# A two-layer hybrid decoder trunk on one core: first loads, the first norm, and the order of the first products

## The chip, the cores and the metric

The kernel runs on one core of a Trainium2 chip. The metric is the time of one execution in microseconds on the device. The kernel before took 1389.82 us, the median of three runs (1389.7 to 1390.5). A core has five engines that run side by side, each with its own queue of instructions in a fixed order: TensorE (PE in the profile; its weight loads are PEld), VectorE (DVE), ScalarE (ACT), GpSimd (POOL) and SyncE (SP), which here issues nearly all transfers from main memory. Semaphores tie them together.

## The reference

A sequence of 512 tokens of width 1024 is normalised and goes through two layers. Each is a mixer (attention with eight query heads in two key/value groups, beside a short gated convolution) and a feed-forward block, dense in layer 0 and with eight experts in layer 1. Cut to what matters here:

```python
def layer_norm(x, g, b):
    mu = jnp.mean(xf, -1, keepdims=True)
    var = jnp.mean(jnp.square(xf - mu), -1, keepdims=True)
    return ((xf - mu) * lax.rsqrt(var + LN_EPS) * g + b).astype(x.dtype)
...
def hybrid_mixer(h, w_in, ...):
    z = h @ w_in
    q, kc, vc, ks, vs, kw, vw, gates, u, bg, cg = jnp.split(z, offsets, axis=-1)
    kc_c = compress(kv(kc), ...)
    vc_c = compress(kv(vc), ...)
    ...
def reference(x, ln_in_g, ln_in_b, ...):
    h = layer_norm(x, ln_in_g, ln_in_b)
    for l in range(DEPTH):
        m = hybrid_mixer(h, ...)
        h = layer_norm(ALPHA * h + m, ln1_g[l], ln1_b[l])
        f = swiglu(h, ...) if l % 2 == 0 else moe_swiglu(h, ...)
        h = layer_norm(ALPHA * h + f, ln2_g[l], ln2_b[l])
    return h
```

Of z the change touches kc and vc (keys and values that are compressed in blocks) and ks and kw (keys of the selected blocks and of the window). These four, 128 columns each, are the "first projections" of a layer.

## The kernel before

The activations h stay on chip as four blocks of 128 tokens (`NT` = 4) by 1024. Every wide product is made of three: an operand x is split into a high half xh (a reduced format that TensorE multiplies quickly) and a low half xl, the rest; a weight w likewise into whi and wlo. Then x w is xh whi + xl whi + xh wlo, summed in one bank of PSUM. `split` (L136) makes the weights' halves: whi on ScalarE (L142), wlo on DVE or, for the first projections of layer 0, on POOL (L143). `split_t` (L175) transposes one block of h on TensorE into a bank of the kind "tr" (L183), and takes xh from it on ScalarE (L187) and xl on DVE (L188).

There are eight banks of PSUM: two "mm", two "tr", three "s" and one "po". A tile that takes a bank again waits until the bank's last reader is done. Weights come in through a ring of three buffers, "stage"; the halves whi and wlo have rings of four each. The program is written in order, but a scheduler places the instructions on the engines' queues; what it made of them is seen in the rows of the section on the change.

Head (L60 to L105, and `run`, L1092): `setup` issues, in this order, blocks 0 and 1 of x, ln_in_g, ln_in_b, the first weights `st0` (the 256 columns of kc and vc, 1 MB), and blocks 2 and 3 of x. `mixer` adds `st2` (ks and kw) behind them. Then small constants are made (an identity for the transposes, masks). `run` normalises the four blocks: two `bn_stats` of 512 columns on DVE (`ln_stats`, L159), their aggregate (L166), a square root on ScalarE (L167), a reciprocal (L168), and two passes over the block, (x - mean) g (L925) and times 1/sigma plus b (L926), then `split_t`.

First projections (`proj_first`, L209): four weights, four banks (mm, mm, s, s). The tokens are taken in two halves of 256 (`th`), so that work can start when two of the four blocks are ready. In a half, one projection after the other, and within it for each of the eight slices of 128 rows (`KD` = 8) the three products xh whi, xl whi, xh wlo: 24 matmuls of 256 columns a projection, 96 a half, 192 in all. It is called in three places: the mixer of layer 0, the first step of the feed-forward block of layer 0 (L600; there the four are two pairs of gate and up columns), and the mixer of layer 1.

After it, in `mixer` (L252), the four banks `pf[0]` to `pf[3]` are read. pf[0] and pf[1] (kc, vc) go into the tiles e_0 and e_1: for each of two groups g and each of two offsets, two copies of 64 partitions from ScalarE (r = 0, L302) and two from DVE (r = 1, L304). pf[2] and pf[3] (ks, kw) become ks on ScalarE (L282, and L285 for the other half of the partitions) and the rest kl on DVE, eight instructions of 64x512 (L284). In layer 0 `columns` (L119) transposes a tile of constants on TensorE into an mm bank (L122), and copies it to `cols` (L124). Then come q's projections (`proj_t`, 24 matmuls of 512 columns each, mm banks) and `compress` (L361), whose first products (L373) read e_0.

Of the kernel before, what the change touches and what calls it, by code (L numbers as in the profile page):

```python
# [7 lines left out]
F32 = mybir.dt.float32  # L8
F32R = mybir.dt.float32r
BF = mybir.dt.bfloat16  # L10
F16 = mybir.dt.float16
I32 = mybir.dt.int32
AF = mybir.ActivationFunctionType
OP = mybir.AluOpType
# [3 lines left out]
S, D, NT, KD = 512, 1024, 4, 8  # L18
# [28 lines left out]
C_KC, C_VC, C_KS, C_VS, C_KW, C_VW, C_G, C_U, C_B, C_C = 512, 640, 768, 896, 1024, 1152, 1280, 1304, 1816, 2328  # L47


class Trunk:  # L50
# [9 lines left out]
    def setup(self):  # L60
        nc, t = self.nc, self.t
        self.const = self.pool("const")
        self.state = self.pool("state")
        self.ring = self.pool("ring", 2)
        self.small = self.pool("small", 4)
        c = self.const
        self.h = self.state.tile([128, NT, D], F32, name="h")
        self.gb = self.ring.tile([128, 2, D], F32, name="stage", bufs=3)
        for tt in range(NT):
            nc.sync.dma_start(self.h[:, tt], t["x"][0, tt * 128:(tt + 1) * 128])  # L70
            if tt == 1:
                self.ln_load(self.gb, t["ln_in_g"], t["ln_in_b"])
                self.st0 = self.block([128, KD, 256], lambda s: [(s, self.win(0, C_KC, 256))])
        self.eps = c.tile([128, 1], F32, name="eps")
        nc.vector.memset(self.eps, EPS)
        early = self.state.tile([128, 2, 128], I32, name="xl")
        jp, jc = early[:, 0], early[:, 1].rearrange("p (t n) -> p t n", t=NT)
        nc.gpsimd.iota(jp, pattern=[[1, 128]], base=0, channel_multiplier=-1)
        self.ident = c.tile([128, 128], F32, name="ident")
        nc.vector.tensor_scalar(self.ident, jp, 0.0, None, op0=OP.is_equal)  # L80
        self.identb = c.tile([128, 128], BF, name="identb")
        nc.vector.tensor_copy(self.identb, self.ident)
        self.cneg = c.tile([128, 128], BF, name="cneg")
        nc.vector.tensor_scalar(self.cneg, jp, 0.0, NEG, op0=OP.is_gt, op1=OP.mult)
        self.fold = c.tile([128, 64], F32, name="fold")
        nc.vector.tensor_tensor(self.fold, self.ident[:, 0:64], self.ident[:, 64:128], op=OP.add)
        nc.gpsimd.iota(jc, pattern=[[-128, NT], [16, 32]], base=31, channel_multiplier=-1)
        self.nneg = c.tile([128, NT, 32], BF, name="nneg")
        nc.vector.tensor_scalar(self.nneg, jc, 0.0, NEG, op0=OP.is_gt, op1=OP.mult)
        self.nkeep = c.tile([128, NT, 32], BF, name="nkeep")  # L90
        nc.vector.tensor_scalar(self.nkeep, jc, 0.0, None, op0=OP.is_le)
        self.nkeep8 = c.tile([128, 8, 8], BF, name="nkeep8")
        nc.gpsimd.memset(self.nkeep8, 0.0)
        for e in range(1, NE):
            nc.gpsimd.memset(self.nkeep8[:, e, 0:e], 1.0)
        self.before = c.tile([128, 128], BF, name="before")
        nc.vector.tensor_scalar(self.before, jp, 0.0, None, op0=OP.is_gt)
        self.ones = c.tile([128, 128], BF, name="ones")
        nc.vector.memset(self.ones, 1.0)
        self.slots = c.tile([128, CAP], F16, name="slots")  # L100
        nc.gpsimd.iota(self.slots, pattern=[[1, CAP]], base=1, channel_multiplier=0, allow_small_or_imprecise_dtypes=True)
        self.toks = c.tile([128, NT], F16, name="toks")
        nc.gpsimd.iota(self.toks, pattern=[[128, NT]], base=0, channel_multiplier=1, allow_small_or_imprecise_dtypes=True)
        self.dump = c.tile([128, 2], F32, name="dump")
        nc.gpsimd.iota(self.dump, pattern=[[CH, 2]], base=S, channel_multiplier=1, allow_small_or_imprecise_dtypes=True)  # L105

    def columns_load(self, ip):

        nc, t = self.nc, self.t
        rows = ip.tile([128, 128], F32, name="rows")  # L110
        nc.gpsimd.memset(rows, 0.0)
        nc.sync.dma_start(rows[0:64], t["cmp_pos"].rearrange("l k (c r) d -> (l k c) (r d)", r=2))
        nc.sync.dma_start(rows[64:88], t["conv_w"].rearrange("l k (j p) -> (l k j) p", p=128))
        nc.sync.dma_start(rows[88:96], t["cmp_b1"].rearrange("l k (m p) -> (l k m) p", p=128))
        for r in range(2):
            nc.sync.dma_start(rows[96:100, r * 64:(r + 1) * 64], t["cmp_b2"].rearrange("l k d -> (l k) d"))
        return rows
# [43 lines left out]
    def ln_rows(self, x, st, gb):  # L161

        nc = self.nc
        m = x.shape[0]
        mv, rs = (self.small.tile([128, n], F32, name=name)[0:m] for name, n in (("mv", 2), ("rs", 1)))
        nc.vector.bn_aggr(mv, st)  # L166
        nc.scalar.activation(rs, mv[:, 1:2], AF.Sqrt, bias=self.eps[0:m])  # L167
        nc.vector.reciprocal(rs, rs)  # L168
        self.rows_scaled(x, mv[:, 0:1], rs, gb)
        return mv  # L170
# [38 lines left out]
    def proj_first(self, sts, engs=(None,) * 4):  # L209

        ws = [tuple(self.split(st, 128, eng=eng)) for st, eng in zip(sts, engs)]
        ps = [self.psum(tag) for tag in ("mm", "mm", "s", "s")]
        for th in range(2):
            q = slice(th * 256, th * 256 + 256)
            for (hi, lo), p in zip(ws, ps):
                self.mm3(p[:, q], lambda k: (hi[:, k], lo[:, k], self.xh[:, k, q], self.xl[:, k, q]), 0, KD)
        return ps

    def rows_out(self, nk, load, act, gb, after):
# [872 lines left out]
    def run(self):  # L1092
        self.ps = self.pool("ps", 1, PSUM)
        self.setup()
        gb = self.gb
        for tt in range(NT):
            for half in range(2):
                self.ln_stats(tt, half)
            self.ln_norm(tt, gb)
            self.split_t(tt)  # L1100
        for l in range(DEPTH):
            if l % 2 == 0:
                self.mixer(l, self.split_t)
                self.ffn(l)
            else:
                rp = self.pool("route%d" % l)
                dp = self.ctx.enter_context(self.tc.tile_pool(name="moed%d" % l, bufs=1, space=bass.MemoryType.DRAM))
                self.hbuf = dp.tile([S, D], F32, name="hbuf")
                self.abuf = dp.tile([S + CAP, D], F32, name="abuf")
                self.route(l, rp)  # L1110

                def after(tt):
                    for rows in (self.hbuf, self.abuf):
                        self.nc.gpsimd.dma_start(rows[tt * 128:(tt + 1) * 128], self.h[:, tt])
                    self.route_tile(tt)
                self.mixer(l, after)
                self.moe(l)
# [32 lines left out]
```

## Time and profile before

| | us |
|---|---|
| median of the runs | 1389.82 (1389.7 to 1390.5) |
| the profiled execution | 1391.8 |
| its span, first to last instruction | 1389.8 |
| TensorE busy | 1339.5 |
| DVE busy | 867.3 |
| ScalarE busy | 670.0 |
| POOL busy | 75.1 |
| layer 0: first transposes start | 11.91 |
| layer 0: first products start | 17.05 |
| layer 0: second half of tokens starts | 34.53 |
| layer 0: first projections end, columns' transpose starts | 45.89 |
| layer 0: q's projections start | 46.48 |
| layer 1: q's projections start | 669.89 |

The profile is of one execution, and the times in it count from the start of its span. Matmuls are pipelined: the step from one start to the next (0.12 us for 256 columns) is what one costs, not its own duration (0.28).

### The profile page before, as it was taken

To read this page: it belongs to the slowest core of one execution; us is meant where nothing else is said; L and a number is where in the kernel's file an instruction comes from. 1 tells how busy PE (TensorE), PEld (TensorE's weight loads), DVE (VectorE), ACT (ScalarE), POOL (GpSimd) and SP (SyncE) were. 2 spreads that over 40 slices of the span, in tenths; PEclk is the share of its full clock that TensorE was granted. 3 is DMA by queue.
4 is the path that set the end of the run, shared out by engine and by line. 5 is a ranking of instruction groups with operands and counts; after the bars stand their busy time and mean duration, and the time that the engine had idled before them with its cause. 6 is when DMAs were issued, how large, how long until landed. Compare 5 with 4: busy or idle time off the path is not lost.

```text
span 1389.8 us, 27646 instructions
## 1 busy us (share of the span) xinstructions
PE 1339.5 (96%) x11888; PEld 1181.5 (85%) x11888; DVE 867.3 (62%) x1249; ACT 670.0 (48%) x951; POOL 75.1 (5%) x81
## 2 busy tenths in 40 slices
PE   5999999999999999999999999999999999999974
PEld 5887888898888888888888878889999999999974
DVE  7567665843333332228567665769787788778876
ACT  3575544332322322122565444236777677668761
POOL 3000000000000000000000000101101140011010
PEclk9999999999999999999999999999999999999986
DMA  7442021232322322234442021679999999999961
GB/s 249 128 121 62 31 61 61 91 122 72 110 92 90 121 92 91 91 107 110 130 122 62 32 61 61 211 270 321 327 356 334 323 332 389 337 363 353 343 236 75
DMA packets 135810, 241.16 MB, mean 174 GB/s; under 512 B 10810, under 2 KB 80538, under 8 KB 135684
## 3 DMA queue, kind: packets, MB, share of 16 engines
q1 hardware_dynamic: 131444, 225.28, 47.5%
q0 software_dynamic: 4240, 14.07, 3.7%
q8 instruction: 94, 1.54, 0.5%
q14 instruction: 32, 0.26, 0.1%
HBM read 227.74 MB, written 11.68 MB: 172 GB/s over the span
## 4 chain that ended last, share of the span: by engine, by line
PE 91%; DVE 4%; DMA 2%; ACT 1%; issue 1%; SPq 0%; POOL 0%; POOLq 0%; ACTq 0%
PE mm L198 46%; PE s L198 17%; PE tr L198 11%; PE po L481 3%; PE s L499 2%; PE s L465 2%; PE s L373 1%; PE po L198 1%; PE tr L465 1%; PE tr L499 1%; DVE h L925 1%; PE tr L183 1%; DVE h L926 1%; PE mm L677 1%; PE po L475 1%
## 5 line engine op out<-in xcount | busy, mean ns | idle before, releaser
L198 PEld LDWEIGHTS <-whi 128*128 128x128 f16 x4224 | 342.8, 99 | 2.9 <-issue 2.4
L142 ACT ACTIVATE whi<-stage 128x1024 fp32r<-128x1024 f32 x122 | 127.9, 1058 | 304.8 <-PE mm L198 181.7
L143 DVE TENSOR_TENSOR wlo<-stage,whi 128x1024 fp32r<-128x1024 f32 x118 | 143.7, 1223 | 196.6 <-ACT whi L142 194.4
L198 PE MATMUL mm<-xh,whi 128*128 128x512 f32 (+1 forms) x672 | 257.4, 383 | 0.3 <-DVE e L304 0.3
L198 PE MATMUL mm<-xh,wlo 128*128 128x512 f32 (+1 forms) x672 | 253.0, 377 | 0.4 <-DVE wlo L143 0.4
L198 PE MATMUL mm<-xl,whi 128*128 128x512 f32 (+1 forms) x672 | 252.3, 376 | 0.0
L825 DVE SCALAR_TENSOR_TENSOR wlo<-estage,whi 128x1536 f16<-128x1536 f32 (+4 forms) x106 | 201.6, 1919 | 35.2 <-ACT whi L824 34.9
L198 PEld LDWEIGHTS <-wlo 128*128 128x128 f16 x2112 | 208.6, 99 | 13.2 <-DVE wlo L825 13.2
L824 ACT ACTIVATE whi<-estage 128x1536 f16<-128x1536 f32 (+4 forms) x106 | 170.6, 1613 | 68.8 <-PE s L198 28.0
L198 PEld LDWEIGHTS mm<-xh,wlo 128*128 128x128 f32 x672 | 127.1, 189 | 24.0 <-DVE wlo L143 0.6
L198 PEld LDWEIGHTS mm<-xh,whi 128*128 128x128 f32 x672 | 127.6, 190 | 21.6 <-issue 1.3
L198 PEld LDWEIGHTS mm<-xl,whi 128*128 128x128 f32 x672 | 127.3, 189 | 21.1
L198 PE MATMUL tr<-eh,wlo 128*128 128x128 f16 (+6 forms) x704 | 136.2, 228 | 8.3 <-DVE wlo L825 8.3
L198 PE MATMUL s<-ehh,wlo 128*128 128x128 f16 (+6 forms) x704 | 134.7, 228 | 4.5 <-DVE wlo L825 4.5
L198 PE MATMUL tr<-eh,whi 128*128 128x128 f16 (+6 forms) x704 | 136.3, 229 | 0.0
L198 PE MATMUL tr<-el,whi 128*128 128x128 f16 (+6 forms) x704 | 136.2, 228 | 0.0
L198 PE MATMUL s<-ehh,whi 128*128 128x128 f16 (+6 forms) x704 | 134.7, 228 | 1.1 <-ACT ehh L865 1.1
L198 PE MATMUL s<-ehl,whi 128*128 128x128 f16 (+6 forms) x704 | 134.6, 228 | 1.1 <-DVE ehl L866 1.1
L198 PE MATMUL mm<-eh,whi 128*128 128x128 f16 (+6 forms) x704 | 132.7, 226 | 0.0
L198 PE MATMUL mm<-el,whi 128*128 128x128 f16 (+6 forms) x704 | 132.6, 226 | 0.0
L198 PE MATMUL mm<-eh,wlo 128*128 128x128 f16 (+6 forms) x704 | 132.6, 226 | 0.0
L825 DVE SCALAR_TENSOR_TENSOR wlo<-stage,whi 128x1536 f16<-128x1536 f32 (+5 forms) x56 | 103.0, 1842 | 23.2 <-ACT whi L824 22.2
(302 smaller groups left out, 2220.7 us busy)
## 6 DMA issues: line engine op xcount, KB each, us to landing
estage<-in_moe_wd_dram SPq DMA_DIRECT2D x29, 1024.0 KB, 7.7
stage<-in_w_in_dram SPq DMA_DIRECT2D x32, 512.0 KB, 5.1
estage<-in_moe_wu_dram SPq DMA_DIRECT2D x21, 768.0 KB, 10.5
estage<-in_moe_wg_dram SPq DMA_DIRECT2D x18, 768.0 KB, 7.1
stage<-in_ffn_wg_dram SPq DMA_DIRECT2D x11, 1024.0 KB, 5.2
stage<-in_ffn_wu_dram SPq DMA_DIRECT2D x11, 1024.0 KB, 5.2
stage<-in_ffn_wd_dram SPq DMA_DIRECT2D x11, 1024.0 KB, 4.8
stage<-in_moe_wd_dram SPq DMA_DIRECT2D x11, 1024.0 KB, 9.4
```

The costliest lines, as they stand in the source:

```text
L142: nc.scalar.activation(h, st, AF.Copy)
L143: (eng or nc.vector).tensor_tensor(o, st, h.bitcast(F32), op=OP.subtract)
L183: nc.tensor.transpose(p[:, k * 128:(k + 1) * 128], self.h[:, tt, kk * 128:(kk + 1) * 128], self.ident)
L198: self.nc.tensor.matmul(p, a, b, start=first and n == 0, stop=last and n == total - 1, skip_group_check=shared)
L373: nc.tensor.matmul(ph[r:r + 64, 0:256], e2[kv][:, c].rearrange("p g n -> p (g n)"), w1s[c // 8][:, c % 8], start=c < 2, stop=c > 13, skip_ ...
L465: nc.tensor.transpose(q[:, k * 128:k * 128 + 128], flat[:, c:c + 128], self.ident)
L475: nc.tensor.matmul(po, vbd[r], pct[r, la // 2], start=True, stop=False, skip_group_check=True)
L481: nc.tensor.matmul(po[g * 64:g * 64 + 64, i * 128:i * 128 + 128], v[:, j, c:c + 64], flat[:, k:k + 128], start=False, stop=lbr == 1 and j ...
L499: nc.tensor.matmul(sp[:, wide[i]], qs[:, a, g, qi[i]], keys[:, br, g, 0:wide[i].stop - wide[i].start], start=keys is ks and i == blocks[0] ...
L677: self.nc.tensor.matmul(p, self.h[:, tt, k * 128:k * 128 + 128], self.oh32[:, tt], start=tt == 0 and k % 3 == 0, stop=tt == NT - 1 and (k ...
L824: nc.scalar.activation(hi[:, c], st[:, c], AF.Copy, scale=WS)
L825: self.low = nc.vector.scalar_tensor_tensor(lo[:, c], st[:, c], WS, hi[:, c], op0=OP.mult, op1=OP.subtract)
```

## The change

Four things are done. The loads move from `setup` into `loads`, called after the constants; in it st0 comes behind all four blocks of x, where it stood ahead of blocks 2 and 3. The first norm moves into `first_norm`: blocks 0 and 1 as before, with their statistics placed after the last constant on DVE (`issue_after`, which sets an order on the queue); blocks 2 and 3 get their sum and the sum of squares from two passes on ScalarE that accumulate (placed after the last square root of blocks 0 and 1), with the mean and the square root there too, and the two scaling passes on DVE as before. In `proj_first`, in each half of the tokens, the products with whi of all four projections come first (64 matmuls), and the products with wlo of all four last (32). As `proj_first` is shared, this holds at all three of its places.

```diff
--- before.py
+++ after.py
@@ -64,13 +64,6 @@
         self.ring = self.pool("ring", 2)
         self.small = self.pool("small", 4)
         c = self.const
-        self.h = self.state.tile([128, NT, D], F32, name="h")
-        self.gb = self.ring.tile([128, 2, D], F32, name="stage", bufs=3)
-        for tt in range(NT):
-            nc.sync.dma_start(self.h[:, tt], t["x"][0, tt * 128:(tt + 1) * 128])
-            if tt == 1:
-                self.ln_load(self.gb, t["ln_in_g"], t["ln_in_b"])
-                self.st0 = self.block([128, KD, 256], lambda s: [(s, self.win(0, C_KC, 256))])
         self.eps = c.tile([128, 1], F32, name="eps")
         nc.vector.memset(self.eps, EPS)
         early = self.state.tile([128, 2, 128], I32, name="xl")
@@ -94,7 +87,7 @@
         for e in range(1, NE):
             nc.gpsimd.memset(self.nkeep8[:, e, 0:e], 1.0)
         self.before = c.tile([128, 128], BF, name="before")
-        nc.vector.tensor_scalar(self.before, jp, 0.0, None, op0=OP.is_gt)
+        self.made = nc.vector.tensor_scalar(self.before, jp, 0.0, None, op0=OP.is_gt)
         self.ones = c.tile([128, 128], BF, name="ones")
         nc.vector.memset(self.ones, 1.0)
         self.slots = c.tile([128, CAP], F16, name="slots")
@@ -103,6 +96,42 @@
         nc.gpsimd.iota(self.toks, pattern=[[128, NT]], base=0, channel_multiplier=1, allow_small_or_imprecise_dtypes=True)
         self.dump = c.tile([128, 2], F32, name="dump")
         nc.gpsimd.iota(self.dump, pattern=[[CH, 2]], base=S, channel_multiplier=1, allow_small_or_imprecise_dtypes=True)
+
+    def loads(self):
+        nc, t = self.nc, self.t
+        self.h = self.state.tile([128, NT, D], F32, name="h")
+        self.gb = self.ring.tile([128, 2, D], F32, name="stage", bufs=3)
+        for tt in range(NT):
+            nc.sync.dma_start(self.h[:, tt], t["x"][0, tt * 128:(tt + 1) * 128])
+            if tt == 1:
+                self.ln_load(self.gb, t["ln_in_g"], t["ln_in_b"])
+        self.st0 = self.block([128, KD, 256], lambda s: [(s, self.win(0, C_KC, 256))])
+
+    def first_norm(self):
+
+        nc = self.nc
+        with ExitStack() as ctx:
+            lp = self.pool("first", 1, ctx=ctx)
+            scratch = lp.tile([128, D], BF, name="scratch")
+            s = lp.tile([128, NT, 4], F32, name="sums")
+            for tt in range(2):
+                with self.tc.issue_after(self.made.ins):
+                    for half in range(2):
+                        self.ln_stats(tt, half)
+                self.ln_norm(tt, self.gb)
+            for tt in range(NT):
+                x = self.h[:, tt]
+                if tt > 1:
+                    total, mean, var, rs = (s[:, tt, i:i + 1] for i in range(4))
+                    with self.tc.issue_after(self.root.ins):
+                        nc.scalar.activation(scratch, x, AF.Copy, accum_out=total)
+                    nc.scalar.activation(mean, total, AF.Copy, scale=-1.0 / D)
+                    nc.scalar.activation(scratch, x, AF.Square, bias=mean, accum_out=var)
+                    nc.scalar.activation(rs, var, AF.Sqrt, bias=self.eps, scale=1.0 / D)
+                    nc.vector.reciprocal(rs, rs)
+                    nc.vector.scalar_tensor_tensor(x, x, mean, self.gb[:, 0], op0=OP.add, op1=OP.mult)
+                    nc.vector.scalar_tensor_tensor(x, x, rs, self.gb[:, 1], op0=OP.mult, op1=OP.add)
+                self.split_t(tt)
 
     def columns_load(self, ip):
 
@@ -164,7 +193,7 @@
         m = x.shape[0]
         mv, rs = (self.small.tile([128, n], F32, name=name)[0:m] for name, n in (("mv", 2), ("rs", 1)))
         nc.vector.bn_aggr(mv, st)
-        nc.scalar.activation(rs, mv[:, 1:2], AF.Sqrt, bias=self.eps[0:m])
+        self.root = nc.scalar.activation(rs, mv[:, 1:2], AF.Sqrt, bias=self.eps[0:m])
         nc.vector.reciprocal(rs, rs)
         self.rows_scaled(x, mv[:, 0:1], rs, gb)
         return mv
@@ -212,8 +241,13 @@
         ps = [self.psum(tag) for tag in ("mm", "mm", "s", "s")]
         for th in range(2):
             q = slice(th * 256, th * 256 + 256)
-            for (hi, lo), p in zip(ws, ps):
-                self.mm3(p[:, q], lambda k: (hi[:, k], lo[:, k], self.xh[:, k, q], self.xl[:, k, q]), 0, KD)
+
+            for low in range(2):
+                for (hi, lo), p in zip(ws, ps):
+                    for k in range(KD):
+                        for a, b in (((lo, self.xh),) if low else ((hi, self.xh), (hi, self.xl))):
+                            self.nc.tensor.matmul(p[:, q], a[:, k], b[:, k, q], start=not low and k == 0 and b is self.xh,
+                                                  stop=low == 1 and k == KD - 1)
         return ps
 
     def rows_out(self, nk, load, act, gb, after):
@@ -1092,12 +1126,8 @@
     def run(self):
         self.ps = self.pool("ps", 1, PSUM)
         self.setup()
-        gb = self.gb
-        for tt in range(NT):
-            for half in range(2):
-                self.ln_stats(tt, half)
-            self.ln_norm(tt, gb)
-            self.split_t(tt)
+        self.loads()
+        self.first_norm()
         for l in range(DEPTH):
             if l % 2 == 0:
                 self.mixer(l, self.split_t)
```

**TensorE in the head of layer 0.** The names: tr is a bank of transposes, each row x4 one half of a block; mm is the bank of a projection. Before:

```order
L183 MATMUL tr<-ident,h 128x128 x16
L198 MATMUL mm<-xh,whi 128x256 x2
L198 MATMUL mm<-xl,whi 128x256
L198 MATMUL mm<-xh,wlo 128x256
L198 MATMUL mm<-xh,whi 128x256
L198 MATMUL mm<-xl,whi 128x256
L198 MATMUL mm<-xh,wlo 128x256
```

Now:

```order
L212 MATMUL tr<-ident,h 128x128 x16
L249 MATMUL mm<-xh,whi 128x256 x2
L212 MATMUL tr<-ident,h 128x128 x4
L249 MATMUL mm<-xl,whi 128x256
L249 MATMUL mm<-xh,whi 128x256
L212 MATMUL tr<-ident,h 128x128 x4
L249 MATMUL mm<-xl,whi 128x256
```

The transposes of block 2 (the two rows x4) moved up: they stand behind two products.

**DVE behind the first projections of layer 0**, from the first split of q's weights to the copy of the columns. Before:

```order
L143 TENSOR_TENSOR wlo<-stage,whi 128x1024
L304 COPY e_0_231<-mm 64x8x31 x2
L333 TENSOR_TENSOR ol<-stg,oh 128x8x24
L143 TENSOR_TENSOR wlo<-stage,whi 128x1024
L304 COPY e_0_231<-mm 64x8x31 x2
L304 COPY e_1_232<-mm 64x8x31 x2
L284 TENSOR_TENSOR kl<-s,ks 64x512 x2
L304 COPY e_1_232<-mm 64x8x31 x2
L124 COPY cols<-mm 128x100
L284 TENSOR_TENSOR kl<-s,ks 64x512 x4
L143 TENSOR_TENSOR wlo<-stage,whi 128x1024 x2
L284 TENSOR_TENSOR kl<-s,ks 64x512 x2
```

Now:

```order
L172 TENSOR_TENSOR wlo<-stage,whi 128x1024
L338 COPY e_0_231<-mm 64x8x31 x2
L338 COPY e_1_232<-mm 64x8x31 x2
L318 TENSOR_TENSOR kl<-s,ks 64x512 x8
L338 COPY e_0_231<-mm 64x8x31 x2
L338 COPY e_1_232<-mm 64x8x31 x2
L153 COPY cols<-mm 128x100
L172 TENSOR_TENSOR wlo<-stage,whi 128x1024 x3
```

The eight kl now stand together, ahead of the last four copies of e; before, six of them stood behind all copies of e. In layer 1 the rows are the same without the columns.

**TensorE at the end of the first projections of layer 1.** Before:

```order
L198 MATMUL s<-xh,wlo 128x256
L198 MATMUL s<-xh,whi 128x256
L198 MATMUL s<-xl,whi 128x256
L198 MATMUL s<-xh,wlo 128x256
L198 MATMUL mm<-xh,whi 128x512
L198 MATMUL mm<-xl,whi 128x512
```

Now:

```order
L249 MATMUL s<-xh,whi 128x256
L249 MATMUL s<-xl,whi 128x256
L249 MATMUL mm<-xh,wlo 128x256 x16
L249 MATMUL s<-xh,wlo 128x256 x16
L407 MATMUL s<-stage,e_0_4884 64x256
L227 MATMUL mm<-xh,whi 128x512
L227 MATMUL mm<-xl,whi 128x512
```

The low products of all four projections moved to the end, and one product of `compress` (L407, which reads e_0) moved ahead of q's first product, the first row with 512 columns. In layer 0 the columns' transpose stands in that place, before and now.

## Prediction

> **What bounds the kernel now.** I read the page first, then the list of what TensorE waits for, then three places in order of time.
>
> ```profile
> span 1389.8 us, 27646 instructions
> ...
> PE 1339.5 (96%) x11888; PEld 1181.5 (85%) x11888; DVE 867.3 (62%) x1249; ACT 670.0 (48%) x951; POOL 75.1 (5%) x81
> ...
> PE   5999999999999999999999999999999999999974
> ...
> PE 91%; DVE 4%; DMA 2%; ACT 1%; issue 1%; SPq 0%; POOL 0%; POOLq 0%; ACTq 0%
> ```
>
> TensorE is busy in 96% of the span, and in all slices but the first and the last two it leaves nothing idle; 91% of the chain that ended last lies on it. So time that is added to TensorE's path between about 35 and 1340 us has nowhere to be absorbed, and the same holds for time saved. What the change can win are waits of TensorE, and these are few:
>
> ```profile
> PE tr L183 <- DVE h L926: 14.6, 4, 11.9
> ...
> PE tr L183 <- DVE xl L188: 1.2, 1, 1.2
> ...
> PE mm L198 <- DVE wlo L143: 0.4, 1, 0.4
> PE mm L198 <- DVE e L304: 0.3, 1, 0.3
> ```
>
> Of the 14.6 us, 11.9 are the start. All that TensorE waits for in the three places where `proj_first` runs is in these four rows: about 4.6 us beside the start. That is the most that the new product order and norm together could win without moving the first transposes.
>
> **The head.** The kernel starts with DVE's norm. These are rows of the timeline (start, duration, engine, line, and in brackets the idle time before), of windows of one us (the last number is GB/s), and one of the chain.
>
> ```profile
> 8.43 1.28 DVE L925 SCALAR_TENSOR_TENSOR h<-h,mv,stage 128x1024 f32<-128x1024 f32 x1 [0.91 <-DMA stage<-in_ln_in_g_dram]
> 9.63 0.22 DVE L80 TENSOR_SCALAR ident<-xl 128x128 f32<-128x128 int32 x1
> 9.77 0.22 DVE L84 TENSOR_SCALAR cneg<-xl 128x128 bf16<-128x128 int32 x1
> ...
> 11.91 1.97 PE L183 MATMUL tr<-ident,h 128*128 128x128 f32 x8 [11.91 <-DVE h L926]
> ...
> 13.06 0.60 ACT L187 ACTIVATE xh<-tr 128x512 fp32r<-128x512 f32 x1 [5.24 <-PE tr L183]
> ...
> 10.00:11.00 1.00, 0.00 (x0) 0.00 (x0) 1.00 (x6) 0.00 (x0) 0.00 (x0) 1.00 1.12 365
> ...
> 12.00:13.00 1.00, 1.00 (x5) 1.00 (x6) 1.00 (x1) 0.00 (x0) 0.00 (x0) 1.00 1.00 396
> ...
> 14.69 11.36 POOL L143 TENSOR_TENSOR wlo<-stage,whi 128x1024 fp32r<-128x1024 f32 x4 [12.18 <-ACT whi L142]
> ...
> 21.00 2.81 DVE L926 SCALAR_TENSOR_TENSOR h<-h,rs,stage 128x1024 f32<-128x1024 f32 x1
> ...
> 29.88 1.06 PE L183 MATMUL tr<-ident,h 128*128 128x128 f32 x8 [1.02 <-DVE h L926]
> ...
> 34.53 5.65 PE mm L198 x47
> ```
>
> In the last row, of the chain, the second half of tokens starts: the point at which I compare. Removed from DVE's path before the first transposes are seven constants, which now run before x lands (0.14 us apart: 9.63, 9.77); but block 0's second scaling also needs ln_in_b, one transfer behind ln_in_g. So the first transposes come near 11.2 instead of 11.91: -0.7. Against it, the first weight block (1.05 MB) now queues behind blocks 2 and 3 of x (1.05 MB). ln_in_g ends the wait at 8.43; behind it stood ln_in_b and the weights, 1.57 MB at about 385 GB/s, so 12.5; now it is 2.62 MB, so 15.2 (an estimate from the GB/s column). ScalarE's first split of weights then ends near 16.8, and the first product starts near 17.3.
>
> ScalarE's statistics of 128x1024 have no row in this trace. The nearest are its weight split of the same size, 1.06 us (row 298.59 below), and the copy of 512 columns at 13.06, 0.60; I take 1.06, with bounds of 0.6 and 2.1. Block 2 lands near 11.1, so its mean and sum of squares are there before 13.7 (15.7 at the upper bound), while DVE reaches its scaling only at about 15.6, after two blocks' scalings (4 x 1.28 from 8.43, with the wait for ln_in_b) and block 0's low halves. They are hidden. The scaling itself is not: one of block 2's two and both of block 3's now fall beside POOL's split, where the row at 21.00 shows 2.81 in place of 1.28. Block 2 is ready near 19.4, and its transposes stand in TensorE's queue behind only two products. They start at about 20.0, after DVE's next low half frees the bank. From there: 94 products at 0.12 (the step from 45.77 to 45.89 below; 11.3), 16 transposes (2.1 by the row at 29.88), and a wait of some 1.4 for block 3, whose scalings (2.4 and 2.8) and the low halves between them end near 26.7. That makes 34.8 against 34.53: **+0.2**, with bounds of -3.5 (three scalings at 1.28) and +3 (each at its slowest, and the first dozen products slow). The good cover, TensorE busy with high products while POOL splits, is spent on a later start.
>
> **The tail in layer 0.** Here are DVE, ScalarE and TensorE, where the four first projections end.
>
> ```profile
> 39.71 0.73 DVE L304 COPY e<-mm 64x248 f32<-64x248 f32 x2
> ...
> 41.36 1.23 DVE L143 TENSOR_TENSOR wlo<-stage,whi 128x1024 fp32r<-128x1024 f32 x1 [0.53 <-ACT whi L142]
> ...
> 44.17 1.38 DVE L284 TENSOR_TENSOR kl<-s,ks 64x512 fp32r<-64x512 f32 x2
> 45.58 0.75 DVE L304 COPY e<-mm 64x248 f32<-64x248 f32 x2
> ...
> 46.81 2.81 DVE L284 TENSOR_TENSOR kl<-s,ks 64x512 fp32r<-64x512 f32 x4 [0.18 <-ACT ks L282]
> ...
> 43.20 0.59 ACT L282 ACTIVATE ks<-s 64x512 fp32r<-64x512 f32 x1 [0.56 <-PE s L198]
> ...
> 45.77 0.28 PE L198 MATMUL s<-xh,wlo 128*128 128x256 f32 x1
> 45.89 0.27 PE L122 MATMUL mm<-ident,rows 128*128 128x128 f32 x1
> 46.48 0.47 PE L198 MATMUL mm<-xh,whi 128*128 128x512 f32 x1 [0.32 <-DVE e L304]
> ```
>
> Before, pf[0] is complete 8.6 us before the end (72 products of 0.12), so its copies into e_0 run at 39.71 under the other projections' products; only the last pair of copies of e_1 (45.58) holds TensorE, for 0.32 us. After, the low products of all four stand last: pf[0] to pf[3] complete at T-2.9, T-1.9, T-1.0 and T, where T is the end. DVE's order (in the section on the change) is then: weight split, two pairs of e copies for group 0, eight kl, two pairs of e copies for group 1. Nothing of this can start before T-2.9. Added up: T-2.9, 1.2 for the split, 0.75 and 0.75 for group 0's copies, T-0.15; eight kl at 1.40 a pair, 5.6, T+5.45; group 1's two pairs, T+7.0; and 0.1 for the signal. q's first product takes pf[1]'s bank and the columns' transpose takes pf[0]'s, so q starts at T+7.1. Before it was T+0.59. **+6.5.** Nothing covers it: TensorE's queue holds only these.
>
> Behind the waiting product stand the 48 products of q and then compress; their weights are split long before, and the next weight loads, freed by a split that now comes about 12 us later, still land some microseconds ahead of their use.
>
> **The same in layer 1.**
>
> ```profile
> 654.48 1.06 PE tr L183 x8
> ...
> 669.77 0.28 PE L198 MATMUL s<-xh,wlo 128*128 128x256 f32 x1
> 669.89 0.40 PE L198 MATMUL mm<-xh,whi 128*128 128x512 f32 x1
> ```
>
> Before, q starts with no wait at T = 669.89. After, DVE has the same order, and in front of q stands now one product of compress that reads e_0; it was always to be done (0.2 us), so the loss is 7.1 - 0.2 = **+6.9**. At this layer's head TensorE has 78 instead of 71 first-half products to do before it needs block 3 (654.48): seven more at 0.12 fill the waits there: **-0.8** (0 to -0.9, the two waits of that place).
>
> **The feed-forward block** calls `proj_first` once, too.
>
> ```profile
> 296.79 1.28 ACT L604 ACT_TABLE_LOAD x1
> 298.09 0.60 ACT L604 ACTIVATE g<-mm 128x512 f32<-128x512 f32 x1
> 298.59 1.06 ACT L142 ACTIVATE whi<-stage 128x1024 fp32r<-128x1024 f32 x1
> ```
>
> The fourth weight split on ScalarE waits for the last high product, T-3.8; with 1.06, 1.28 and 0.60 the first bank is read at T-0.9, before the next product needs it. The second bank is needed 5.6 us later. **0**, with up to +1 if the table load comes late.
>
> **The clock after an idle TensorE.** Waits as long as seven us stand only at the end of this trace:
>
> ```profile
> 1340.00:1341.00 1.00, 1.00 (x22) 1.00 (x20) 1.00 (x2) 0.98 (x2) 0.00 (x0) 1.00 1.04 381
> ...
> 1349.96 0.29 PE L198 MATMUL tr<-eh,wlo 128*128 128x128 f16 x1 [8.32 <-DVE wlo L825]
> ...
> 1351.00:1352.00 1.00, 1.00 (x12) 1.00 (x11) 1.00 (x2) 1.00 (x1) 0.00 (x0) 0.50 0.00 0
> ...
> 1354.00:1355.00 1.00, 1.00 (x14) 1.00 (x13) 1.00 (x2) 0.29 (x1) 0.00 (x0) 0.65 0.00 0
> ...
> 1366.20 0.29 PE L198 MATMUL s<-ehh,wlo 128*128 128x128 f16 x1 [4.51 <-DVE wlo L825]
> ...
> 1371.00:1372.00 1.00, 1.00 (x14) 1.00 (x13) 0.00 (x0) 0.00 (x0) 0.00 (x0) 0.61 0.00 0
> ```
>
> The column before the DMA's share is the granted clock. After 8.32 us idle it is 0.50 until about 1354.7 (4.7 us), after 4.51 us idle until about 1371.8 (5.6 us); 12 matmuls a microsecond stand against 22. At half speed that loses 2.35 and 2.8 us, by the counts 2.0 and 2.4; I take 2.3 for each of the two tails, **+4.6**, bounded by 0 and 5.6. The new idle times (about 6 us) lie between the two seen.
>
> The Trainium skill, "TensorE: Matmul & The Clock Gate", section "What's actually happening", says that the clock falls to half after an idle window of about 3.4 us and returns after about 3.4 us of steady work. By its figure the two tails would lose 1.7 us each, an estimate, and the sum would be 1.2 us less; the rows above show longer slow stretches, and I go by them.
>
> **The sum:** 0.2 + 6.5 - 0.8 + 6.9 + 0 + 4.6 = 17.4 us on the span of 1389.8, so 1407.2. The profiled execution itself took 1391.8, 2.0 more than its span; the median of the runs shown is 1389.82, level with the span by chance, so I forecast 1389.82 + 17.4, about **1407 us**.
>
> **Rivals.** (1) The clock does not fall in one or both tails, because the idle stretch is cut by the columns' transpose or lies badly to whatever measures activity: 1402.5 to 1405. For it speaks that no idle time of this size in mid-kernel is in the trace; against it that 4.51 us sufficed. (2) The tail is longer: each of the four kl pairs also waits for ScalarE's copy ks (0.59 at 43.20; ScalarE alternates copies of e, ks and the crossed ks); if all of it were exposed, 4 x 0.6 a layer, 1412. Against it: the row at 46.81 has four kl in 2.81 with only 0.18 of waiting ahead. (3) It is faster: the head. If POOL does not slow the three scalings, the head wins 3.5 and layer 1's head 0.9. That decides only if the two tails together cost less than 4.4 us, 2.2 each, or fewer than two of the four kl pairs; with no tail at all it gives 1385.4. It would need group 1's e copies to be free of the eight kl ahead of them, against the order of DVE's queue. (4) The change doesn't do what it says: low products last don't shorten the wait for POOL, since TensorE's waits there were for h, not for wlo (the list of waits has 0.4 us for wlo, in layer 1). That is already in my sum; it gives the same 1407.
>
> **Chances.** Forecast with both slow clocks 0.62 (1404 to 1410 with the head's likely spread); rival 1: 0.20; rival 2: 0.10; rival 3, or tails hidden so far that the result is within the bound: 0.08. Range: down to 1398 (no slow clock, -4.6, with the head at its best, -3.7, gives 1398.9) and up to 1413 (rival 2; or the head at +3, slow clocks of 2.8 and the feed-forward block at +1 give 1412). 0.2% is 2.8 us, about what a measurement of this kernel tells from no change; rival 3 splits evenly below and within it: faster 0.04, same 0.04, slower 0.92.
>
> **What would show it.** In the trace of after: the second half's first product near 34.8 and not 31; q's first product 7 us behind the last low product, released by DVE's e copy; eight kl in a row in front of it; the granted clock at 0.50 for about 5 us behind each of the two gaps; no gap in the feed-forward block; from then on the same length of all stages. The prediction is wrong if q follows within 2 us of T, if the head wins over 3 us, or if a third gap shows.

## The result, and the profile after

| | before | after |
|---|---|---|
| median, us | 1390.23 (five runs) | 1409.4 (1406.28 to 1409.85, five runs) |
| ratio to before | | 1.0123 (95% interval 1.011 to 1.0135) |
| profiled execution, us | 1391.8 | 1406.28 |
| its span, us | 1389.8 | 1404.0 |

The change makes the kernel slower by 1.2%, some 17 us by the ratio (the two medians lie 19 apart). A second measurement on another occasion gave 1.012 (1.0099 to 1.014). The profiled execution is the shortest of the five; the spans of the other four are 1406.9 to 1407.4.

First the page of after, and the list of what TensorE waited for (microseconds in total, times, longest):

```profile
span 1404.0 us, 27652 instructions
...
PE 1342.1 (96%) x11888; PEld 1182.5 (84%) x11888; DVE 862.7 (61%) x1243; ACT 675.2 (48%) x961; POOL 75.6 (5%) x81
```

```profile
PE tr L212 <- DVE h L960: 11.8, 2, 11.5
...
PE mm L151 <- ACT ks L319: 6.7, 1, 6.7
PE s L407 <- ACT ks L319: 6.4, 1, 6.4
```

The waits for h fell from 14.6 to 11.8 us: beside the start they are almost gone, which is what the change in the head was meant to do. But two waits of 6.7 and 6.4 us are new, one in front of the columns' transpose of layer 0 and one in front of compress's first product of layer 1. The busy time hardly differs. The list names ScalarE's ks as what ended them, but by the program TensorE needs the copies into e there, as the timeline of the place shows, VectorE first and TensorE behind it:

```profile
42.90 1.22 DVE L172 TENSOR_TENSOR wlo<-stage,whi 128x1024 fp32r<-128x1024 f32 x1 [14.25 <-PE mm L249]
44.13 1.38 DVE L338 COPY e<-mm 64x248 f32<-64x248 f32 x4
45.54 2.79 DVE L318 TENSOR_TENSOR kl<-s,ks 64x512 fp32r<-64x512 f32 x4
48.54 2.84 DVE L318 TENSOR_TENSOR kl<-s,ks 64x512 fp32r<-64x512 f32 x4 [0.21 <-ACT ks L316]
51.41 1.42 DVE L338 COPY e<-mm 64x248 f32<-64x248 f32 x4
...
52.37 0.45 PE L151 MATMUL mm<-ident,rows 128*128 128x128 f32 x1 [6.69 <-ACT ks L319]
52.97 0.77 PE L227 MATMUL mm<-xh,whi 128*128 128x512 f32 x1 [0.16 <-DVE e L338]
```

VectorE waited 14.25 us for the first low products to end, and then worked through its queue with one gap of 0.21: a split, four copies, eight kl, four copies. The columns' transpose starts when the first pair of the last four copies is done (near 52.2), q when the second is. The semaphores in the trace bear this out: the long wait in front of the transpose ends at 52.21 on VectorE's semaphore, 0.05 us behind the first pair's end (52.16), while ks was done at 52.00; in layer 1 TensorE's queue moves on 0.04 us behind the first of those copies (683.68), with ks still running (to 683.85). The chain that ended last, piece by piece, gives the stages' sizes, first after, then before:

```profile
34.16 3.84 PE mm L249 x32
...
52.97 12.95 PE mm L227 x48
...
662.80 1.06 PE tr L212 x8
...
666.01 3.84 PE mm L249 x32
...
685.02 12.69 PE mm L227 x48
697.71 3.60 PE s L407 x30
```

```profile
46.48 11.17 PE mm L198 x48
...
658.53 5.76 PE mm L198 x48
...
670.05 10.91 PE mm L198 x48
680.96 3.60 PE s L373 x32
```

The second half of tokens starts at 34.16 and its 96 products end at 45.68 (34.16 + 11.52), so q starts 7.29 us behind the end of the last; before, 0.43 (46.48 against 45.77 + 0.28). q's 48 products take 12.95 us where they took 11.17. At block 3's transposes in layer 1 after is 8.32 us late (662.80 against 654.48), so the feed-forward block has added nothing. Then layer 1's second half is only 7.48 late (666.01 against 658.53), q 14.97 late (685.02 against 670.05), and the products of compress behind it 16.75 (697.71 against 680.96). By the end the two profiled executions differ by 14.2 only; the last section comes to that.

The clock is seen in windows of one microsecond (the column before the DMA's share):

```profile
50.00:51.00 1.00, 0.00 (x0) 0.00 (x0) 0.99 (x2) 0.57 (x1) 0.00 (x0) 0.52 0.00 0
...
53.00:54.00 1.00, 1.00 (x3) 0.81 (x4) 0.97 (x2) 0.00 (x0) 0.81 (x1) 0.50 0.00 0
...
56.00:57.00 1.00, 1.00 (x4) 0.74 (x4) 0.00 (x0) 0.00 (x0) 0.00 (x0) 0.57 1.07 320
```

It falls to half 4.4 us after TensorE stopped, while it still idles, and is back near 56.9, 4 us after q began. In layer 1 it falls 4.0 us after the last product (681.50 against 677.53).

### The profile page after: what moved, and what is told of

Same layout as the page of the kernel before. It is cut to its first block, busy times and chain, and to the rows that moved or that the text cites. A ratio compares the mean times of both kernels' runs of the same rounds, so it can differ in the third digit from the quotient of the medians.

```text
span 1404.0 us, 27652 instructions
## 1 busy us (share of the span) xinstructions
PE 1342.1 (96%) x11888; PEld 1182.5 (84%) x11888; DVE 862.7 (61%) x1243; ACT 675.2 (48%) x961; POOL 75.6 (5%) x81
## 4 chain that ended last, share of the span: by engine, by line
PE 91%; DVE 3%; ACT 2%; DMA 2%; issue 1%; SPq 0%; POOL 0%; POOLq 0%; ACTq 0%
PE mm L227 44%; PE s L227 15%; PE tr L227 11%; PE po L515 3%; PE s L533 2%; PE mm L249 2%; PE s L249 2%; PE s L499 1%; PE s L407 1%; PE po L227 1%; PE tr L499 1%; DMA abuf<-yr,dst 1%; PE tr L533 1%; PE tr L212 1%; DMA h<-in_x_dram 1%
## 5 line engine op out<-in xcount | busy, mean ns | idle before, releaser
L227 PE MATMUL mm<-xh,whi 128*128 128x512 f32 x576 | 231.3, 402 | 0.2 <-DVE e L338 0.2
L227 PE MATMUL mm<-xh,wlo 128*128 128x512 f32 x576 | 226.4, 393 | 0.0
L227 PE MATMUL mm<-xl,whi 128*128 128x512 f32 x576 | 225.7, 392 | 0.0
L227 PEld LDWEIGHTS mm<-xh,wlo 128*128 128x128 f32 x576 | 109.0, 189 | 23.5
L227 PEld LDWEIGHTS mm<-xh,whi 128*128 128x128 f32 x576 | 109.5, 190 | 22.6 <-issue 1.9
L227 PEld LDWEIGHTS mm<-xl,whi 128*128 128x128 f32 x576 | 109.2, 190 | 21.3
```

The lines of the kernel that those rows point to most:

```text
L227: self.nc.tensor.matmul(p, a, b, start=first and n == 0, stop=last and n == total - 1, skip_group_check=shared)
```

## The experiments

My theory was that of the prediction: low products last make all four banks complete late, VectorE's queue holds eight kl ahead of e's last copies, and the clock falls in the gap. The rivals put the loss into the loads and the norm, into the banks' completion alone, or denied the clock its part. Each ratio below is to the kernel before, run beside it.

**The old product order in the changed kernel.**

```diff
-            for low in range(2):
-                ...
+            for (hi, lo), p in zip(ws, ps):
+                self.mm3(p[:, q], lambda k: (hi[:, k], lo[:, k], self.xh[:, k, q], self.xl[:, k, q]), 0, KD)
```

> The changed kernel with the product order of before in proj_first; loads and first norm stay changed. Theory (the low products at the end make e's copies and kl late, and TensorE's clock falls behind the two gaps): both gaps in front of q go, no half clock near 53 or 685 us, and the time is that of before within 2 us, 1388 to 1392. Rival (the later load of the first weights and the statistics on ScalarE cost it): it stays within 4 us of the changed kernel, 1403 to 1409.

1392.16 us, ratio 1.0008 (0.9998 to 1.0017): the time of before. Its chain:

```profile
33.84 5.66 PE mm L227 x47
...
45.79 11.15 PE mm L227 x48
```

The second half starts 0.7 us earlier than before, as the first transposes do (11.08 against 11.91), and q's products run at full clock. Loads and norm cost nothing that shows, and what they win can't be told in the time.

**The new order alone in the kernel before.** The diff is the other way round.

> The kernel before with only the new product order in proj_first. Theory: the second half of tokens starts where it did (34.5), since 30 low products still stand behind block 3's transposes at 29.9; then 6.7 and 7.5 us of waiting in front of q in layers 0 and 1, 1.8 us each of slow clock, 0.7 won at layer 1's head: 1406 to 1408. Rival (loads and norm cost it): within 3 us of the kernel before.

1407.48 us, ratio 1.0116 (1.0102 to 1.0131): all of the loss, within the noise. The second half starts at 33.96, not at the 34.5 that I expected; the first transposes are as much earlier in this run (11.33 against 11.91). Its list of waits has the same pair, to the tenth:

```profile
PE mm L122 <- ACT ks L290: 6.7, 1, 6.7
PE s L378 <- ACT ks L290: 6.4, 1, 6.4
```

**e's copies written ahead of ks and kl.** In `mixer` the loop over ks and kl moves behind the loop over e:

```diff
-            for i in range(2):
-                ... (ks, kl)
             if l == 0:
                 self.columns(rows)
             for kv in range(2):
                 ...
+            for i in range(2):
+                ... (ks, kl)
```

> The changed kernel with the copies into e written ahead of ks and kl in the mixer; seven of the eight kl then stand behind all copies of e on VectorE. Theory (the wait is VectorE's queue, five and a half us of it kl): q starts some 2.2 us behind the last low product instead of 7.3, the clock stays at 1.00 there, and the time is 1392 to 1395. Rival (the wait is for the banks' completion itself, whatever stands ahead on VectorE): the wait stays above 5 us and the time above 1402.

1394.9 us, ratio 1.0026 (1.0016 to 1.0036). TensorE in layer 0 (its last low product ends at 44.52):

```profile
46.03 0.30 PE L151 MATMUL mm<-ident,rows 128*128 128x128 f32 x1 [1.51 <-ACT ks L336]
46.69 0.50 PE L227 MATMUL mm<-xh,whi 128*128 128x512 f32 x1 [0.35 <-DVE cols L153]
```

q starts 2.17 us behind. The banks complete as late as in the changed kernel, so their late completion alone doesn't make the wait: it takes the kl in front of the copies, seven of which now stand behind them. This order repairs four fifths of the loss, but doesn't beat before: the split of q's weights and the copies themselves still stand there.

**TensorE kept busy in the waits.** Products into the free bank, behind the first projections; their result is not used:

```diff
+            pw = self.psum("po")
+            for i in range(52):
+                nc.tensor.matmul(pw[:, 0:256], self.xh[:, 0, 0:128], self.xh[:, i % 8, 256:512], start=True, stop=True)
```

> The changed kernel with 52 more products of 256 columns into the free po bank (their result is not used), placed behind the last low product in both mixers: 6.2 us of work at full clock inside the waits. Theory (the clock falls because TensorE idles): q still starts some 7 us behind the last low product, but its 48 products take 11.2 us in layer 0 and 10.9 in layer 1 instead of 12.95 and 12.7, and the time is 3.6 us less than the changed kernel's, 1403 to 1406 where that shows 1407 to 1409. Rival (they are slow for another reason, such as late weights): the 48 products still take over 12.5 us and the time doesn't fall.

1405.55 us, ratio 1.0103 (1.0088 to 1.0117). Since the interval meets that of the changed kernel, both went again, on one chip:

> The changed kernel once more, on the same chip as the next run: 1406 to 1410, waits of 6.7 and 6.4 us in front of q in layers 0 and 1, and a granted clock of 0.50 behind each.

> The run with 52 products in each wait once more, beside the changed kernel: 3.4 us less by the traces (1.8 and 1.6 us of slow products), so a ratio to before lower by 0.0024; if the slow clock were harmless, no difference.

The changed kernel 1408.76 us, 1.012 (1.0099 to 1.014); with the 52 products 1405.17, 1.0093 (1.0073 to 1.0112). The ratio is lower by 0.0027 where 0.0024 was expected. The two intervals still overlap, but the runs themselves don't: the fastest of the changed kernel took 1407.94 us, the slowest with the 52 products 1406.7. The traces say the same; timeline and chain of the first of the two runs with the products:

```profile
45.80 6.40 PE L314 MATMUL po<-xh 128*128 128x256 f32 x52
...
53.25 0.47 PE L227 MATMUL mm<-xh,whi 128*128 128x512 f32 x1 [0.30 <-DVE e L341]
```

```profile
53.25 11.14 PE mm L227 x48
```

q starts just as late, but its products take 11.14 us instead of 12.95, in layer 1 11.14 instead of 12.69. Doing useless work makes the kernel faster: with the idle time filled, q's products take what they took before (11.17), so the slow products come from the idle time.

**Half of it.** The same with `range(26)`.

> As the run with 52 products in the two waits, with 26: TensorE works 3.1 us behind the last low product and then idles some 3.7 us. By the rows so far the clock fell 4.2 and 4.8 us after TensorE stopped and held through 2.2 us; if it needs over 4 us of idle time the granted clock stays at 1.00 in both waits and q's products take 11.2 us; if 3.7 us are enough it shows 0.50 and they take 12.0 to 12.9.

One run, 1410.95 us, with no interval. The longer branch of what I expected failed: 3.57 us of idle time in layer 0 and 3.29 in layer 1 are enough.

```profile
684.39 1.09 PE L410 MATMUL s<-stage,e 128*64 128x256 f32 x2 [3.29 <-ACT ks L322]
```

```profile
52.00:53.00 1.00, 0.65 (x2) 0.46 (x3) 0.76 (x3) 0.00 (x0) 0.36 (x3) 0.85 0.00 0
...
683.00:684.00 1.00, 0.00 (x0) 0.00 (x0) 0.97 (x2) 0.28 (x1) 0.00 (x0) 1.00 0.00 0
684.00:685.00 1.00, 0.61 (x2) 0.29 (x2) 1.00 (x4) 0.31 (x1) 0.00 (x0) 0.58 0.00 0
...
687.00:688.00 1.00, 1.00 (x5) 0.82 (x4) 0.00 (x0) 0.00 (x0) 0.00 (x0) 0.71 0.24 41
```

By its share of those microseconds the clock falls in layer 1 at 684.16, 0.2 us before TensorE resumes, and stays at half for 3.4 us (to 687.58). In layer 0 it falls at 52.70, 0.7 us after TensorE resumed (51.96), and q's products take 12.78.

**Low products last in the first half of tokens only.** In the second half each projection takes its three products together, in the changed kernel:

```diff
+            if th == 1:
+                for (hi, lo), p in zip(ws, ps):
+                    self.mm3(p[:, q], lambda k: (hi[:, k], lo[:, k], self.xh[:, k, q], self.xl[:, k, q]), 0, KD)
+                continue
             for low in range(2):
```

> The changed kernel with the low products last only in the first half of the tokens; in the second half each projection takes its three products as before. Theory (the loss lies in the second half's end alone, where the banks complete): q starts 0.6 us behind the columns' start in layer 0 and with no wait in layer 1, no half clock there, layer 1's head still wins 0.7, the first head 0.4 to 0.7: 1388 to 1390 where before shows 1390, a difference below what can be told. Rival (the new order costs something in the first half or the feed-forward block too): over 1392.

and in the kernel before:

> The kernel before with the low products last only in the first half of the tokens; loads and norm as before. Theory: the second half starts near 34.0 instead of 34.5 as in the run with the new order alone, 0.7 won in layer 1, no tails: 1388 to 1390. If the loads and the norm on ScalarE are worth anything in time, the run with them and the same order is faster than this one by more than 0.5 us; I expect less than that.

1391.13 us, 0.9988 (0.9976 to 1.0001), and 1390.83 us, 0.9992 (0.9977 to 1.0006). The tails are gone from both. The chain of the first:

```profile
33.98 5.66 PE mm L227 x47
...
45.93 11.13 PE mm L227 x48
```

In layer 1, q starts at 668.52 in it and at 668.75 in the other, against 670.05 in the chain of before: 1.5 and 1.3 us won by both heads together, some 0.1%, which the times don't tell from nothing. Between them, loads and norm make no difference that shows.

**The first weights ahead of blocks 2 and 3 again**, with the same product order:

> As the run with the low products last in the first half only, and the first weights loaded ahead of blocks 2 and 3 of x again. Theory (the later weights hold TensorE's first products, whose second waited 0.95 us for the weight split of ScalarE): first products near 16 instead of 17.5, the second half of tokens 1 to 2.5 us earlier than 34.2 and the time 1386 to 1388.5. Rival (what counts is block 3's scaling beside POOL's split, now earlier): the second half starts within 0.5 us of 34.2, no gain.

1396.04 us, 1.0028 (1.0017 to 1.0039): slower, and for a reason that neither side had named. ScalarE and VectorE:

```profile
12.19 1.06 ACT L171 ACTIVATE whi<-stage 128x1024 fp32r<-128x1024 f32 x1 [5.10 <-DMA stage<-in_w_in_dram]
13.15 0.28 ACT L196 ACTIVATE rs<-mv,eps 128x1 f32<-128x1 f32 x1
...
13.47 0.16 DVE L197 RECIPROCAL rs<-rs 128x1 f32<-128x1 f32 x1 [2.82 <-ACT rs L196]
13.55 3.21 DVE L963 SCALAR_TENSOR_TENSOR h<-h,mv,stage 128x1024 f32<-128x1024 f32 x1
```

The scheduler placed a weight split in front of block 1's square root, on ScalarE; the split waited for its load until 12.19, and block 1's norm with it. Its scaling then ran beside POOL's splits, at 3.21 us instead of 1.27. So I placed the four splits behind that square root:

```diff
+                with self.tc.issue_after(self.root.ins):
+                    ws.append(tuple(self.split(st, 128, eng=eng)))
```

> As the run with the first weights loaded ahead of blocks 2 and 3, with ScalarE's first four weight splits placed behind block 1's square root. Theory (there the 8 us were lost because block 1's square root stood behind a weight split that waited for its load): the wait of 8 us in front of block 1's transposes goes. Block 3's scaling then falls beside POOL's split, ends near 29, and 31 low products stand behind its transposes: second half of tokens at 33.3 to 34.5, time 1388 to 1391, no gain over the run without the earlier load. Rival (the later load was what cost): second half before 33, time under 1388.

1391.16 us, 0.9994 (0.9981 to 1.0007). The loss is gone, and with it any gain: the second half starts at 34.69, a little later than expected, since the weights' low halves on POOL now meet VectorE's scaling of block 3:

```profile
24.18 2.99 DVE L132 SCALAR_TENSOR_TENSOR h<-h,sums,stage 128x1024 f32<-128x1024 f32 x1 [0.34 <-ACT scratch L129]
```

No version that was run beats the kernel before by more than can be measured.

## Why the prediction was right

The forecast of 1407 us and its mechanism held. Term by term, in the chain of after against that of before:

| term | forecast, us | measured, us | from |
|---|---|---|---|
| head, to the second half of tokens | +0.2 | -0.4 | 34.16 against 34.53 |
| tail, layer 0 | +6.5 | +6.9 | 7.29 against 0.43 |
| clock, layer 0 | +2.3 | +1.8 | 12.95 against 11.17 |
| feed-forward block | 0 | 0 | 8.32 late = -0.4 + 6.9 + 1.8 |
| head, layer 1 | -0.8 | -0.8 | 8.32 late, then 7.48 |
| tail, layer 1 | +6.9 | +7.5 | 7.48 late, then 14.97 |
| clock, layer 1 | +2.3 | +1.8 | 12.69 against 10.91 |
| sum | 17.4 | 16.8 | |

The two tails were forecast from VectorE's order and the rows of before to within 0.6 us. In layer 1 the wait was 6.4 us, and the two products of compress behind it, at half clock, took 1.08 (0.62 at full clock, with e's copies first). I had priced them at 0.2 and taken that off as work that falls away later; but the 30 that are left take 3.60 us, as the 32 did. That the sum came within a microsecond is partly luck: the clock was put 1.0 too high, the tails 1.0 too low.

**The head came out small by terms that were wrong.** I put block 2's second scaling and both of block 3's beside POOL, at 2.4 to 2.8 us. Block 2's took 1.28 and block 3's 1.45 and 1.72, so block 3 was ready in time and the wait of 1.4 us did not come. In its place stood ScalarE: the second product waited 0.95 us (until 19.08) for the second of the weight splits, which stood behind the statistics in ScalarE's queue; block 2's transposes still started at 19.66 instead of 20.0. And the first products were slow: they step by 0.21 us or more until 22.66, by 0.12 from there, which I had only in the upper bound; it makes about 1.1 us (an estimate: 94 products at 0.12 and two blocks of transposes at 1.06 from 19.66 would end at 33.1, not at 34.16). The head came out at -0.4 where I had +0.2: the sign was the other one, inside bounds as wide as -3.5 to +3.

**The clock's term was mis-sized**: 1.8 instead of 2.3. The half clock lasted less long under q than in the rows that I went by: 3.9 us in layer 0 (52.97 to 56.86) and 3.4 in layer 1 (684.95 to 688.32), against 4.7 and 5.6. And a product of 512 columns takes 0.43 us at it (53.54 to 53.97 in the timeline) against 0.23: 1.9 times, not quite twice. The estimate of 1.7 us a tail from the Trainium skill's figure ("TensorE: Matmul & The Clock Gate", section "What's actually happening") was the nearer one. Its idle window of about 3.4 us is near what the run with 26 products shows, where the clock fell with an idle time of 3.57 us and also with one of 3.29, and stayed at half for 3.4.

Of the rivals, the first (no slow clock) fell to the clock's rows. The second, a tail that waits for ks at each step, did not show: VectorE waited 0.21 us for it. The third (POOL spares the scalings) came in part, but could not weigh against two tails. The fourth holds: waits for low halves weren't what TensorE stood for, and the order that avoids them won nothing in the head. Counted from the first transposes, the second half starts 22.6 us later in the kernel before and with the new order alone, 22.7 in the changed kernel and 22.8 in it with the old order.

## What to carry to other kernels

When products are reordered so that work which is ready early goes first, ask what the last product of each bank releases: finishing four banks together moves all their readers behind the end, and the readers' queue, in its own order, becomes the path. Let the order follow the need in each part: low halves last where they are late (the first half of tokens), bank by bank where the readers wait (the second). Here that cost nothing, but it won nothing that shows either. And price an idle TensorE with its clock: here waits of 6.4 and 6.7 us made the 48 products behind them 1.8 us slower, waits of 3.3 and 3.6 us made them 1.2 and 1.6 slower, and one of 2.2 us left their pace at 0.23.

## What the runs showed of the hardware that I had not expected

**The clock can fall after the fact.** With 26 products in the wait, the granted clock of layer 0 was 1.00 all through an idle time of 3.57 us and dropped 0.7 us after TensorE was at work again. A gap can thus cost although the clock in it looks whole; with 2.2 us (e's copies first) it stayed at 1.00.

**The half clock comes in steps of 3.4 us.** Every stretch of it that starts between 40 and 1375 us in these traces lasts 3.4, 6.8 or 10.2 us: 3.4 with 26 products (684.16 to 687.58), 6.8 in the profiled run of after (50.04 to 56.86), 10.2 in the kernel before (1344.46 to 1354.70, by the windows of its first and last microsecond). A stretch costs only what of it lies under work: of the 6.8 us of after, 2.9 passed before q began.

**It also fell where TensorE never stopped.** In the profiled execution of before:

```profile
1241.00:1242.00 1.00, 1.00 (x6) 0.64 (x5) 1.00 (x1) 0.47 (x2) 0.00 (x0) 1.00 1.11 425
...
1243.00:1244.00 1.00, 1.00 (x10) 1.00 (x11) 1.00 (x3) 0.41 (x1) 0.73 (x1) 0.50 1.00 383
...
1246.00:1247.00 1.00, 1.00 (x21) 1.00 (x19) 0.00 (x0) 0.06 (x1) 0.00 (x0) 1.00 1.03 401
```

TensorE is busy throughout, yet runs at half clock for 3.4 us (1242.06 to 1245.48). In the profiled execution of after no such stretch stands at that place, and its lag shrinks there from 16.4 to 15.2 us, and to 14.2 by the end. This is how 16.8 us at 700 become 14.2 at the end of these two executions, while the ratio of all runs stands for 17.

The traces show what goes ahead of such a stretch. From 1239.33 to 1242.92 TensorE does nothing but 16 transposes of 80x80 for one expert (L794). Between 950 and 1300 us ten stretches start in six of the runs' traces, and each starts during the last four of such a row of 16 or within 1 us behind it. Not every row is followed by one: in after, none stands behind the row from 1256.20 to 1259.41. What decides between the two is open, and so is whether the transposes set it off.

**VectorE's scaling beside POOL varies more than one row tells**: the same 128x1024 instruction took 1.28, 1.45, 1.72, 2.99 and 3.21 us in these runs, according to where it fell among POOL's splits. A single slow row, as the 2.81 that I went by, is no price for the next order.
